# Macaron encoder trunk on one core: weights split by VectorE or by DMAs after a table, first inner tile in eight pieces, a new order

## The chip, the cores and the metric

The kernel runs on 1 core of one Trainium2 chip. The metric is the device time of one execution in microseconds; lower is better. A core has TensorE (PE in the profile; its weight loads are PEld), VectorE (DVE), ScalarE (ACT), GpSimd (POOL) and SyncE (SP). In this kernel SyncE and GpSimd issue all DMAs, GpSimd those that add into their target.

## What is computed

Two layers act on x of 512 frames by 1024 channels: a half-step SwiGLU, a mixer of parallel head groups, another half-step SwiGLU, and at the end a last RMSNorm.

```python
def reference(x, ...):
    for l in range(DEPTH):                                     # DEPTH = 2
        x = x + 0.5 * swiglu(rms_norm(x, ffn1_norm[l]), ffn1_w_in[l], ffn1_w_out[l])
        x = x + hybrid_mixer(rms_norm(x, mix_norm[l]), mix_w_in[l], ..., mix_w_out[l], pos)
        x = x + 0.5 * swiglu(rms_norm(x, ffn2_norm[l]), ffn2_w_in[l], ffn2_w_out[l])
    return rms_norm(x, final_norm)

def swiglu(h, w_in, w_out):                                    # D_FF = 2816
    gate, up = jnp.split(h @ w_in, 2, axis=-1)
    return (jax.nn.silu(gate) * up) @ w_out

def hybrid_mixer(h, w_in, ...):                                # columns of h @ w_in:
    y_conv = conv_module(u_conv, ...)        # GLU, causal depthwise conv (31 taps), LayerNorm, swish
    y_sb = stick_breaking(q_sb, k_sb, v_sb)  # 8 heads of 64
    y_r = silu(g_r) * head_norm(retention(rotary(q_r), rotary(k_r), v_r))   # 4 heads of 64
    return jnp.concatenate([y_conv, y_sb, y_r], axis=-1) @ w_out
```

All of it is float32.

## The kernel before

x stands in SBUF transposed, as eight tiles of 128 channels by 512 frames. A float32 product is made of three float32r products: each operand is split into a high part (hi, the rounded value) and the rest (lo), and hi·hi, hi·lo and lo·hi are added up in PSUM (`product`, lines 357 to 374; `block`, 523 to 538).

**Splitting a weight.** A weight unit is 128x1024 (w_in, mixer) or 128x768 and 128x640 (w_out of the half-steps). There are two ways. `weight` (line 348, `load` and `parts`): SyncE fetches it into `w_raw`, ScalarE casts it to `w_hi` (L320), VectorE subtracts to make `w_lo` (L323). `weight_by_dma` (line 339): GpSimd fetches it straight into `w_hi` (L343), ScalarE writes its negative into `w_lo` (L344), and a second DMA from GpSimd adds the weight from HBM onto it (L345). The second way needs no VectorE and reads the weight twice. Before, only the plain w_in tiles below go by DMA, 30 units in all.

**A half-step** (`ffn`) works on 22 tiles f of 128 inner channels. The first PLAIN = 4 are plain: gate and up are accumulated over the eight x tiles, in 48 products of 512 columns (`pf`), two weight units each, and the norm's factor is multiplied in afterwards (`gated`, L611 and L614). The other 18 go through `inner`, a 2x2 block scheme with seven block products instead of eight: 84 products of 256 columns (`pr`, `pu`), with sums of weight blocks, of which one is made by an adding DMA from GpSimd (L548, `w_raw`) and two by VectorE (L556). Their right-hand sides B and T are made once per half-step by `forms` (L496 to L516), and need the norm's factor `rstd`. The inner tiles are summed in four parts (PARTS) into `po` with w_out; after the last part x gets its `xh`, `xl` and square for the next norm.

**The norm** is a chain: squares summed on PE (`ss`, L462), `ms` on VectorE, a power on GpSimd (`rt`, L428), `dg` on VectorE (L440), a spreading product on PE (`bc`, L451), a copy to `rstd` on ScalarE (L470).

**The mixer** has the projections (`pj`, `pv`), the heads (`z`, ScalarE's exponentials, `y`), the conv's 31 taps on VectorE (`yc`, L1043), its LayerNorm at the end (`cmu`, `cvs`, `cbc`) and the output product in two halves (`mo`): the first half's four inputs are ready early, the second half's late.

**What sets the order.** No instruction is placed by hand. `Plan.add` records every operation with an engine and a cost, and `Plan.forward` plays them through: on every engine the lowest rank whose inputs are ready and whose buffer is free goes next. The rank is the place in the program plus `late` (DENSE_LATE for the mixer's dense products, TAPS_LATE for the conv's taps). The costs, among them the time from a DMA's issue to its landing, decide which operation the plan takes for ready; the resulting order is then fixed on every engine, and each engine works through its own list in order. Buffers are slots of rooms: 9 tiles for w_hi and w_lo, 2 for w_raw, 7 for block sums, PSUM banks 3 (mm), 4 (z) and 1 (y).

## Time and profile before

| | |
|---|---|
| time, median of 3 runs | 2015.3 us (2011.3 to 2019.25) |
| the profiled execution | 2015.95 us, its span 2014.1 us |
| mean granted TensorE clock in it | 0.974 |
| first mixer's norm sums (`ss`) | at 387.8 us |
| second half-step of layer 0, its `ss` | at 660.3 us |
| first half-step of layer 1, its `ss` | at 1014.0 us |
| second mixer's, last half-step's `ss` | at 1374.8 and 1647.0 us |
| HBM read | 268.80 MB, 134 GB/s over the span |
| instructions PE, DVE, ACT, POOL | 11522, 1961, 1534, 153 |

The profile is one execution on the chip. A row of the timeline has the start from the beginning of the span, the duration, engine, line, operation, output and inputs; in brackets the idle time of the engine before it and what ended it. The durations of matmuls overlap, since they are pipelined, so what PE can do is read from the distance of their starts and not from busy time. The view of waits sums up, for each pair of a waiting and a releasing instruction, the idle time in total, how often, and the longest. A window row has, for a stretch of time, each engine's busy time and instructions (x), the granted clock and the DMA share.

### The profile page before, as it was taken

Reading aid. Unit: us, or ns where it says so; the run is one execution under the profiler, and the core shown is the slowest. Engines: PE = TensorE matmul, PEld = TensorE weight load, DVE = VectorE, ACT = ScalarE, POOL = GpSimd, SP = SyncE. Lnnn points to the kernel's source line nnn. Section 1 sums busy time; section 2 is a strip of 40 time slices with the busy share of each in tenths; the row PEclk is TensorE's granted clock in tenths of the full one; section 3 lists DMA queues with packets and bytes.
Section 4 is the critical chain, followed back from the end, with each engine's and each line's share of the span. In section 5 each row is a group of like instructions: output and inputs, shape, how many; then the busy total and the mean of one; then the engine's idle time right before and its main releaser. Section 6 shows DMA issues by size and latency. Waiting matters only on the chain.

```text
span 2014.1 us, 29115 instructions
## 1 busy us (share of the span) xinstructions
PE 1928.1 (96%) x11522; PEld 1712.8 (85%) x11522; DVE 1373.2 (68%) x1961; ACT 973.7 (48%) x1534; POOL 148.1 (7%) x153
## 2 busy tenths in 40 slices
PE   5999999999998999999999999999999899999996
PEld 3989999788876799898779999988877788898995
DVE  5766566568997657666666666656799858565664
ACT  4535344463785434343444344445648654343442
POOL 2000000000002100000120000000000110010000
PEclk8999999999988999999999999999999999999998
DMA  9457564332417656565665565534332373575642
GB/s 268 120 152 190 152 168 140 116 105 73 116 42 174 136 140 180 152 181 144 172 147 147 157 177 154 170 112 122 85 113 64 113 157 100 152 187 152 155 131 69
DMA packets 98393, 281.19 MB, mean 140 GB/s; under 512 B 11472, under 2 KB 11984, under 8 KB 98256
## 3 DMA queue, kind: packets, MB, share of 16 engines
q1 hardware_dynamic: 70032, 210.11, 33.5%
q0 software_dynamic: 28224, 69.21, 18.4%
q8 instruction: 90, 1.47, 0.3%
q14 instruction: 47, 0.39, 0.1%
HBM read 268.80 MB, written 2.10 MB: 134 GB/s over the span
## 4 chain that ended last, share of the span: by engine, by line
PE 79%; DVE 8%; DMA 6%; issue 5%; ACT 1%; SPq 0%; POOL 0%; POOLq 0%; DVEq 0%; ACTq 0%
PE po L369 7%; PE po L368 7%; PE po L370 7%; PE pu L534 6%; PE pu L535 6%; PE pu L536 6%; PE pr L534 4%; PE pr L536 4%; PE pr L535 4%; DMA w_raw<-in_f_in 4%; PE pf L368 3%; PE pf L370 3%; PE pf L369 3%; DVE yc L1043 2%; PE z L876 2%
## 5 line engine op out<-in xcount | busy, mean ns | idle before, releaser
L320 ACT CAST w_hi<-w_raw 128x1024 fp32r<-128x1024 f32 (+2 forms) x338 | 320.3, 948 | 435.1 <-PE pu L535 124.5
L323 DVE TENSOR_TENSOR w_lo<-w_raw,w_hi 128x1024 fp32r<-128x1024 f32 (+2 forms) x338 | 369.7, 1095 | 82.5 <-ACT w_hi L320 62.9
L368 PE MATMUL po<-hh,w_hi 128*128 128x512 f32 x704 | 278.5, 396 | 10.4 <-ACT hh L320 9.6
L369 PE MATMUL po<-hl,w_hi 128*128 128x512 f32 x704 | 278.2, 395 | 1.1 <-DVE hl L323 1.1
L370 PE MATMUL po<-hh,w_lo 128*128 128x512 f32 x704 | 276.8, 393 | 1.9 <-DVE w_lo L323 1.7
L534 PE MATMUL pr<-T_hi,s_hi 128*128 128x256 f32 x576 | 162.7, 282 | 3.8 <-ACT ga L570 3.8
L368 PEld LDWEIGHTS po<-hh,w_hi 128*128 128x128 f32 x704 | 134.2, 191 | 37.0 <-ACT hh L320 10.9
L534 PE MATMUL pu<-B_hi,w_hi 128*128 128x256 f32 x576 | 162.5, 282 | 0.5 <-DVE up L583 0.5
L535 PE MATMUL pu<-B_lo,w_hi 128*128 128x256 f32 x576 | 162.5, 282 | 0.0
L536 PE MATMUL pu<-B_hi,w_lo 128*128 128x256 f32 x576 | 162.3, 282 | 0.0
L535 PE MATMUL pr<-T_lo,s_hi 128*128 128x256 f32 x576 | 162.3, 282 | 0.0
L536 PE MATMUL pr<-T_hi,s_lo 128*128 128x256 f32 x576 | 162.0, 281 | 0.0
L548 POOL DMA_DIRECT2D w_raw<-in_f_in x72 | 85.9, 1239 | 1024.4 <-DMA w_raw<-in_f_in 558.1
L370 PEld LDWEIGHTS po<-hh,w_lo 128*128 128x128 f32 x704 | 133.8, 190 | 31.2 <-DVE w_lo L323 2.7
L647 DVE SCALAR_TENSOR_TENSOR x<-po,x 128x512 f32<-128x512 f32 x128 | 88.2, 690 | 104.7 <-PE po L370 104.3
L369 PEld LDWEIGHTS po<-hl,w_hi 128*128 128x128 f32 x704 | 134.1, 190 | 27.1 <-DVE hl L323 2.6
L590 DVE TENSOR_TENSOR ga<-pu,ga 128x512 f32<-128x512 f32 x72 | 49.7, 691 | 131.4 <-PE pu L536 131.1
L368 PE MATMUL pf<-xh,w_hi 128*128 128x512 f32 x288 | 118.7, 412 | 9.9 <-ACT w_hi L320 9.9
L370 PE MATMUL pf<-xh,w_lo 128*128 128x512 f32 x288 | 115.1, 400 | 5.7 <-DMA w_lo<-in_f_in 5.6
L369 PE MATMUL pf<-xl,w_hi 128*128 128x512 f32 x288 | 114.9, 399 | 0.0
L534 PEld LDWEIGHTS pr<-T_hi,s_hi 128*128 128x128 f32 x576 | 109.3, 190 | 5.1 <-ACT ga L570 4.8
L534 PEld LDWEIGHTS pu<-B_hi,w_hi 128*128 128x128 f32 x576 | 109.4, 190 | 4.2 <-DVE up L583 1.5
(187 smaller groups left out, 4886.0 us busy)
## 6 DMA issues: line engine op xcount, KB each, us to landing
w_raw<-in_f_in SPq DMA_DIRECT2D x218, 512.0 KB, 4.3
w_raw<-in_f_in POOLq DMA_DIRECT2D x72, 512.0 KB, 6.6
w_raw<-in_f_out SPq DMA_DIRECT2D x64, 384.0 KB, 3.3
w_raw<-in_f_out SPq DMA_DIRECT2D x64, 320.0 KB, 3.0
w_raw<-in_m_in SPq DMA_DIRECT2D x36, 512.0 KB, 3.5
w_hi<-in_f_in POOLq DMA_DIRECT2D x30, 512.0 KB, 5.2
w_lo<-in_f_in POOLq DMA_DIRECT2D x30, 512.0 KB, 7.1
w_raw<-in_m_out SPq DMA_DIRECT2D x16, 512.0 KB, 3.6
```

What stands on the lines that cost most here:

```text
L320: self.a(n, lambda: nc.scalar.copy(view(hi), view(src)), [src], [hi])
L323: lambda: nc.vector.tensor_tensor(out=view(lo), in0=view(src), in1=view(hi).bitcast(F32), op=ALU.subtract),
L368: mm(acc[:], hi[:, c], h[:], start=first and a + i == 0, stop=False)
L369: mm(acc[:], hi[:, c], l[:], start=False, stop=False)
L370: mm(acc[:], lo[:, c], h[:], start=False, stop=last and a + i == len(ks) - 1)
L534: mm(out, hi[:, c], h, start=first and j + i == 0, stop=False, **opts)
L535: mm(out, hi[:, c], l, start=False, stop=False, **opts)
L536: mm(out, lo[:, c], h, start=False, stop=j + i == 2, **opts)
L548: lambda: nc.gpsimd.dma_start(rs[:].rearrange("p (a b) -> p a b", a=2), src[:, None, 2 * q : 3 * q].to_broadcast([P, 2, q]), accum_op=ALU.add,
L590: self.v(S, lambda: nc.vector.tensor_tensor(out=ga[:], in0=u[:], in1=ga[:], op=ALU.add), [u, ga], [ga])
L647: lambda x=x, po=po: nc.vector.scalar_tensor_tensor(out=x[:], in0=po[:], scalar=-0.5, in1=x[:], op0=ALU.mult, op1=ALU.add),
L876: nc.tensor.matmul(z[:, c : c + n], m[:], logs[jb][part][:, jc : jc + n], start=False, stop=i == len(todo) - 1 and part == 1, skip_group_c ...
```

## The change

- A table SPLITS gives for each of the six stages (half-step, mixer, half-step, twice) a letter per weight unit, in the order of the program: d for `weight_by_dma`, v for VectorE; units past the end of a string are v. Taken together, 93 units now go by DMA (14, 17, 15, 15, 17, 15), among them some of the mixer's and of w_out's, where there were 30, all plain w_in.
- PLAIN goes from 4 to 6 in every half-step: 16 tiles are left for `inner`.
- The very first w_in tile is loaded in eight pieces of 128x256 between the x tiles, each split by itself (`first_weights`), and ten products on a tile of zeros are put ahead of the first one (`warm`).
- The last norm leaves out the copy of `bc` to `rstd`; VectorE reads it from PSUM.
- The plan's costs: DMAs from GpSimd share the planned bus with SyncE's, other DMA times, 0.119 us for a product of 256 columns, 0.09 us more for `xh`; DENSE_LATE 100 to 240, TAPS_LATE 400 to 380, one more slot in the room f. Every engine's order comes out anew.

```diff
--- before.py
+++ after.py
@@ -24,12 +24,22 @@
 N_UNITS = 24
 EPS = 1e-6
 NEG = -(2.0**100)
-N_F, N_R, N_RAW, N_W, N_WS = 19, 45, 2, 9, 7
-PLAIN = 4
+N_F, N_R, N_RAW, N_W, N_WS = 20, 45, 2, 9, 7
+PLAIN = 6
 AHEAD = 1
-DENSE_LATE, TAPS_LATE = 100, 400
+SPLITS = {
+    0: "dvvvdvdvdvdvddvvvdvvddvvvdvvdvvvvvvvdvvd",
+    1: "vvvdvddvdddvvvvddddvddvdvdddd",
+    2: "dvddvvdvddvvvvvvvdvdvdvvvdvvvdvvvvvdddd",
+    3: "dvddvvdvddvvvvvvvdvdvdvvvdvvvdvvvvvdddd",
+    4: "vvvdvddvdddvvvvddddvddvdvdddd",
+    5: "dvddvvdvddvvvvvvvdvdvdvvvdvvvdvvvvvdddd",
+}
+DENSE_LATE, TAPS_LATE = 240, 380
 PARTS = ((0, 6), (6, 12), (12, 17), (17, 22))
 HS = S // 2
 TT = S // P
@@ -221,7 +231,7 @@
                     cost += LOAD if tables else 0.0
                     tables = o.table
                 o.start, idle[e] = now, now + cost
-                if e == "sync":
+                if isinstance(o.lag, tuple):
                     bus = max(bus, now + cost) + o.lag[0]
                     o.end = bus + o.lag[1]
                 else:
@@ -231,7 +241,7 @@
                 done += 1
                 for a in o.after:
                     left[a] -= 1
-                    t = o.end + (SIGNAL if ops[a].engine != e or e == "sync" else 0.0)
+                    t = o.end + (SIGNAL if ops[a].engine != e or isinstance(o.lag, tuple) else 0.0)
                     ready[a] = max(ready[a], t)
                     if not left[a]:
                         heapq.heappush(queues[ops[a].engine], (rank[a], a))
@@ -297,19 +307,20 @@
         self.tc, self.nc, self.io, self.out = tc, tc.nc, io, out
         self.plan = Plan()
         self.late = 0
+        self.modes = SPLITS[0]
     def v(self, n, fn, r, w, inputs=1, late=0):
         return self.plan.add("vector", vec(n, inputs), fn, r, w, late=late)
-    def a(self, n, fn, r, w, table=None, after=()):
-        return self.plan.add("scalar", sca(n), fn, r, w, table=table, after=after)
+    def a(self, n, fn, r, w, table=None, after=(), more=0.0):
+        return self.plan.add("scalar", sca(n) + more, fn, r, w, table=table, after=after)
     def pe(self, cost, fn, r, w, late=0):
         return self.plan.add("tensor", cost, fn, r, w, lag=0.17, late=late)
     def dma(self, size, fn, r, w):
-        return self.plan.add("sync", 0.33, fn, r, w, lag=(size / 350e3, 1.7))
+        return self.plan.add("sync", 0.33, fn, r, w, lag=(size / 330e3, 1.9))
     def tile(self, room, name, shape=(P, S), dtype=F32):
         return Buf(room, list(shape), dtype, name)
@@ -334,19 +345,23 @@
     def add_dma(self, n, fn, out):
-        self.plan.add("gpsimd", 0.9, fn, [out], [out], lag=n * P * 4 / 250e3 + 4.0)
+        self.plan.add("gpsimd", 1.1, fn, [out], [out], lag=(n * P * 4 / 200e3, 3.8))
     def weight_by_dma(self, src, n=KT * P):
         nc = self.nc
         hi, lo = (self.tile(self.w, name, (P, KT * P), F32R) for name in ("w_hi", "w_lo"))
-        self.plan.add("gpsimd", 0.6, lambda: nc.gpsimd.dma_start(hi[:, :n], src), [], [hi], lag=n * P * 4 / 250e3 + 2.6)
+        self.plan.add("gpsimd", 0.6, lambda: nc.gpsimd.dma_start(hi[:, :n], src), [], [hi], lag=(n * P * 4 / 300e3, 2.9))
         self.a(n, lambda: nc.scalar.activation(lo[:, :n], hi[:, :n].bitcast(F32), ACT.Copy, scale=-1.0), [hi], [lo])
         self.add_dma(n, lambda: nc.gpsimd.dma_start(lo[:, :n], src, accum_op=ALU.add), lo)
         return hi, lo, 0
     def weight(self, src, n=KT * P):
+        by_dma = self.modes[:1] == "d"
+        self.modes = self.modes[1:]
+        if by_dma:
+            return self.weight_by_dma(src, n)
         return (*self.parts(self.load(src, n), n, "w"), 0)
     def parts(self, raw, n, name, room=None):
@@ -396,7 +411,7 @@
         if g is not None:
             xh, xl = (self.tile(self.r2, n, dtype=F32R) for n in ("xh", "xl"))
             self.xs.append((xh, xl))
-            self.a(S, lambda: nc.scalar.activation(xh[:], x[:], ACT.Copy, scale=g[:, d : d + 1]), [x, g.buf], [xh])
+            self.a(S, lambda: nc.scalar.activation(xh[:], x[:], ACT.Copy, scale=g[:, d : d + 1]), [x, g.buf], [xh], more=0.09)
             self.v(
                 S,
                 lambda: nc.vector.scalar_tensor_tensor(
@@ -451,7 +466,7 @@
         self.pe(0.86, lambda: self.nc.tensor.matmul(bc[:], self.ones[:], dg[:], start=True, stop=True), [self.ones, dg], [bc])
         return bc
-    def norm(self, room):
+    def norm(self, room, last=False):
         nc, acc = self.nc, self.acc
         ps = self.bank(room, "ss")
@@ -466,6 +481,9 @@
         self.pe(0.13 * TT * len(acc), sums, [*acc, self.ones], [ps])
         self.r = self.inv_sqrt(ps, TT, 1.0 / D)
         bc = self.spread(self.r, room, "bc")
+        if last:
+            self.rstd = bc
+            return
         rstd = self.rstd = self.tile(self.f2, "rstd")
         self.a(S, lambda: nc.scalar.copy(rstd[:], bc[:]), [bc], [rstd])
@@ -473,11 +491,33 @@
-    def plain(self, src, weight=None):
+    def plain(self, src):
         q = KT * P // 2
-        (h0, l0, _), (h1, l1, _) = ((weight or self.weight)(src[:, c : c + 2 * q]) for c in (0, 2 * q))
+        (h0, l0, _), (h1, l1, _) = (self.weight(src[:, c : c + 2 * q]) for c in (0, 2 * q))
         return [[(h0, l0, 0), (h1, l1, q)], [(h1, l1, 0), (h0, l0, q)]]
+    def first_weights(self, src, j):
+        q, n, out = KT * P // 2, 2 * P, []
+        for block in ((0, 2), (3, 1))[j // 2]:
+            raw, hi, lo = self.tile(self.f2, "wf", (P, n)), *(self.tile(self.r2, f"wf_{p}", (P, n), F32R) for p in ("hi", "lo"))
+            at = block * q + j % 2 * n
+            self.dma(n * P * 4, lambda raw=raw, at=at: self.nc.sync.dma_start(raw[:], src[:, at : at + n]), [], [raw])
+            self.split(raw, n, hi, lo)
+            out.append((hi, lo))
+        return out
+    def warm(self, n):
+        t, ps = self.tile(self.r2, "zeros", dtype=F32R), self.bank(self.y, "warm")
+        self.v(S, lambda: self.nc.vector.memset(t[:].bitcast(F32), 0.0), [], [t])
+        def fn():
+            for i in range(n):
+                self.nc.tensor.matmul(ps[:], t[:, :P], t[:], start=i == 0, stop=i == n - 1)
+        self.pe(0.6 * n, fn, [t], [ps])
     def forms(self, g):
@@ -535,7 +575,7 @@
                     mm(out, hi[:, c], l, start=False, stop=False, **opts)
                     mm(out, lo[:, c], h, start=False, stop=j + i == 2, **opts)
-            self.pe(2 * 3 * HS * COLUMN, fn, [hi, lo, bh, bl], [acc], self.late)
+            self.pe(2 * 3 * 0.119, fn, [hi, lo, bh, bl], [acc], self.late)
     def inner(self, src, b, hs):
@@ -618,10 +658,10 @@
             )
             self.gate(ga, up, pair(f))
-        banks = [self.products(first or self.plain(w_in[0], self.weight_by_dma), (self.mm, self.z))]
+        banks = [self.products(first or self.plain(w_in[0]), (self.mm, self.z))]
         self.norm(self.y)
         for f in range(1, PLAIN):
-            units = self.plain(w_in[f], self.weight_by_dma)
+            units = self.plain(w_in[f])
             accs = [self.bank(room, "pf") for room in (self.mm, self.z)]
             for acc, unit in zip(accs, units):
                 for h in range(2):
@@ -1187,10 +1227,13 @@
             x = self.x[d]
             self.dma(262144, lambda: nc.sync.dma_start(x[:], io["x"][:, d, :]), [], [x])
-        load_x(0)
-        first = self.plain(io["f1_in"][0][0])
-        for d in range(1, KT):
-            load_x(d)
+        self.warm(10)
+        first = [[], []]
+        for j in range(4):
+            load_x(2 * j)
+            for unit, (hi, lo) in zip(first, self.first_weights(io["f1_in"][0][0], j)):
+                unit.append((hi, lo, 0))
+            load_x(2 * j + 1)
         for d in range(KT):
             self.x_ready(d, g[0])
         self.ident = const("ident", [P, P])
@@ -1219,14 +1262,18 @@
         def half_step(name, l, gain, after, first=None):
             self.ws = self.plan.room("ws", N_WS, self.plan.stage, loose=3)
             self.ffn(io[f"{name}_in"][l], io[f"{name}_out"][l], gain, after, first)
+            next_stage()
+        def next_stage():
             plan.next_stage()
+            self.modes = SPLITS.get(plan.stage, "")
         for l in range(DEPTH):
             half_step("f1", l, g[3 * l], lambda d: self.x_ready(d, g[3 * l + 1]), None if l else first)
             self.mixer(l, lambda d: self.x_ready(d, g[3 * l + 2]))
-            plan.next_stage()
+            next_stage()
             half_step("f2", l, g[3 * l + 2], lambda d: self.x_ready(d, g[3 * l + 3] if l < DEPTH - 1 else None))
-        self.norm(self.y)
+        self.norm(self.y, True)
         gl, rstd = g[3 * DEPTH], self.rstd
         for d in range(KT):
             o, x = self.tile(self.f2, f"o{d}"), self.x[d]
```

**GpSimd at the start of the program.** `w_hi` is a fetch, `w_lo` an adding DMA of a weight, `w_raw` the adding DMA of a block sum, `rt` the norm's power. Before:

```order
L343 DMA w_hi<-in_f_in 128x1024 x5
L548 DMA w_raw<-in_f_in 128x2x512 x4
L428 ISA
L428 TENSOR_TENSOR rt<-ms,mhalf 128x4
L345 DMA w_lo<-in_f_in 128x1024 x4
L343 DMA w_hi<-in_f_in 128x1024
```

and now:

```order
L354 DMA w_hi<-in_f_in 128x1024 x4
L354 DMA w_hi<-in_f_out 128x768
L356 DMA w_lo<-in_f_in 128x1024
L588 DMA w_raw<-in_f_in 128x2x512
L443 ISA
L443 TENSOR_TENSOR rt<-ms,mhalf 128x4
L588 DMA w_raw<-in_f_in 128x2x512 x3
```

One adding DMA of a weight has come ahead of the power, and only one block sum is left ahead of it instead of four. On PE, the spreading product `bc` that this power leads to stood directly behind the first tile's 48 products; now 12 products of the second tile, with a weight that VectorE splits, stand between.

**PE at the end of the first half-step of layer 0.** `pu` is the last block product of tile 21, `hh` and `hl` with the numbers 3562 and 3564 (now 3490 and 3498) are that tile's result. Before:

```order
L534 MATMUL pu_3347<-B21_hi_459,w_hi_3279 128x256
L535 MATMUL pu_3347<-B21_lo_489,w_hi_3279 128x256
L536 MATMUL pu_3347<-B21_hi_459,w_lo_3304 128x256
L368 MATMUL po_3434<-hh_3562,w_hi_3327 128x512
L369 MATMUL po_3434<-hl_3564,w_hi_3327 128x512
L370 MATMUL po_3434<-hh_3562,w_lo_3336 128x512
```

and now, from the seventeenth row behind the last `pu`:

```order
L384 MATMUL po_3482<-hl_3447,w_hi_3326 128x512
L385 MATMUL po_3482<-hh_3439,w_lo_3410 128x512
L383 MATMUL po_3399<-hh_3490,w_hi_3233 128x512
L384 MATMUL po_3399<-hl_3498,w_hi_3233 128x512
L385 MATMUL po_3399<-hh_3490,w_lo_3268 128x512
```

Before, the tile's result was needed by the row right behind its last block product; now 18 rows of `po` with older tiles stand between the last `pu` and it.

**PE at the end of the first mixer.** `y` is the last head's product, `cvs` and `cbc` belong to the conv's LayerNorm, `rbc` to the norm of a retention head, `mo` is the output product. Before:

```order
L826 MATMUL y<-wl,vs 128x256
L826 MATMUL y<-wl,vs 128x512
L1069 MATMUL cvs<-avg,csq 128x1 x8
L451 MATMUL cbc<-dg,ones 128x512
L982 MATMUL rbc<-c_ident,ex 128x128 x4
L368 MATMUL mo<-yh,w_hi 128x512
```

and now, around `cbc`:

```order
L916 MATMUL z<-lh,mones 128x128
L916 MATMUL z<-ll,mones 128x128
L466 MATMUL cbc<-dg,ones 128x512
L916 MATMUL z<-lh,r_tri 128x256
L916 MATMUL z<-ll,r_tri 128x256
L916 MATMUL z<-lh,mones 128x128
L916 MATMUL z<-ll,mones 128x128
```

`cvs`, `cbc` and `rbc` have moved ahead of the last head's `y`. 18 rows (12 `mo`, 6 `z`) stand between `cvs` and `cbc`, and 18 more between `cbc` and `rbc`.

## The prediction

> **What bounds the kernel now.** The page's busy line and its chain of waits come first.
>
> ```profile
> PE 1928.1 (96%) x11522; PEld 1712.8 (85%) x11522; DVE 1373.2 (68%) x1961; ACT 973.7 (48%) x1534; POOL 148.1 (7%) x153
> PE 79%; DVE 8%; DMA 6%; issue 5%; ACT 1%; SPq 0%; POOL 0%; POOLq 0%; DVEq 0%; ACTq 0%
> ```
>
> PE is the bound nearly everywhere: 79% of the chain. A change can therefore win in two ways: fewer products, or shorter stretches in which PE waits. VectorE at 68% is relief only where PE waits for it. Those places are in the view of waits, PE's own:
>
> ```profile
> PE pf L368 <- ACT w_hi L320: 9.9, 2, 9.3
> PE po L368 <- ACT hh L320: 9.6, 4, 3.4
> PE bc L451 <- DVE dg L440: 9.3, 2, 6.9
> PE pr L536 <- DVE w_lo L323: 7.2, 2, 3.6
> PE cbc L451 <- DVE dg L440: 6.8, 2, 3.4
> PE z L798 <- ACT wt L842: 5.7, 4, 1.8
> PE pf L370 <- DMA w_lo<-in_f_in: 5.6, 1, 5.6
> PE mo L368 <- ACT yh L320: 4.4, 2, 2.2
> PE ss L462 <- DVE sq L411: 2.8, 2, 2.6
> ```
>
> These are some 61 us, few and long. Each long one is paid a second time, which windows of equal length show.
>
> ```profile
> 363.30:368.30 5.00, 5.00 (x13) 3.94 (x12) 3.16 (x5) 4.26 (x7) 0.57 (x1) 0.50 0.39 105
> 370.00:375.00 5.00, 5.00 (x24) 4.14 (x23) 3.90 (x7) 1.98 (x3) 0.00 (x0) 1.00 0.24 64
> 695.00:700.50 5.50, 1.89 (x9) 1.46 (x9) 5.50 (x9) 2.39 (x4) 0.00 (x0) 0.90 0.00 0
> 700.50:705.50 5.00, 5.00 (x25) 5.00 (x25) 2.15 (x4) 1.42 (x3) 0.00 (x0) 0.50 0.66 194
> 705.50:710.50 5.00, 5.00 (x41) 5.00 (x41) 2.95 (x4) 2.68 (x4) 0.00 (x0) 0.92 0.39 124
> ```
>
> Right after the 3.4 us wait for `hh`, PE gets through 13 matmuls in 5 us, and a little later 24 of the same kind in as long; after the 3.6 us wait for `w_lo`, 25 against 41. So the granted clock was 0.50 for some 5 us behind each. What that costs is the missing matmuls times the distance of two starts, which the timeline of PE gives:
>
> ```profile
> 695.06 0.39 PE L369 MATMUL pf<-xl,w_hi 128*128 128x512 f32 x1
> 695.29 0.39 PE L370 MATMUL pf<-xh,w_lo 128*128 128x512 f32 x1
> ...
> 356.04 0.28 PE L535 MATMUL pu<-B_lo,w_hi 128*128 128x256 f32 x1
> 356.16 0.28 PE L536 MATMUL pu<-B_hi,w_lo 128*128 128x256 f32 x1
> ```
>
> About 0.227 us for 512 columns and 0.119 us for 256 (the rows are rounded to 0.01; these are means over longer stretches). So the first wait costs 3.4 + 11 x 0.227 = 5.9 us, the second 3.6 + 16 x 0.119 = 5.5 us.
>
> The Trainium skill (TensorE: Matmul & The Clock Gate, Part 1: The HAM clock gate) has the clock halved after an idle window of about 3.4 us and back after as long a busy one. By that a wait would cost 1.7 us more, an estimate from the page; the windows show 1.9 and 2.5, and I take theirs. With the page's figure the sum below would gain some 3 us less.
>
> **The change, part by part.** The sum is made against the profiled execution, 2015.95 us (span 2014.1); the median of the runs is 2015.3, which is the same within 0.1%.
>
> *The head of the program: 12 us less.*
>
> ```profile
> 9.30:26.90 17.60, 16.95 (x64) 12.02 (x64) 11.12 (x16) 10.63 (x19) 3.60 (x3) 1.00 1.05 373
> 42.50:47.40 4.90, 4.89 (x12) 3.79 (x13) 4.90 (x10) 0.62 (x1) 0.00 (x0) 0.50 1.06 211
> ...
> 25.48 1.17 POOL L548 DMA_DIRECT2D w_raw<-in_f_in  x1 [0.81 <-DMA w_raw<-in_f_in]
> 27.83 1.50 POOL L428 TENSOR_TENSOR rt<-ms,mhalf 128x4 f32<-128x4 f32 x1
> ...
> 33.00 0.87 DVE L440 TENSOR_SCALAR dg<-c_ident,rt 128x128 f32<-128x128 f32 x4
> 36.77 0.48 DVE L496 SCALAR_TENSOR_TENSOR B<-x,c_gains,rstd 128x256 f32<-128x256 f32 x1 [2.30 <-ACT rstd L470]
> 59.73 0.69 DVE L611 TENSOR_TENSOR ga<-pf,rstd 128x512 f32<-128x512 f32 x1
> ...
> 34.02 2.04 PE L451 MATMUL bc<-dg,ones 128*128 128x512 f32 x2 [6.95 <-DVE dg L440]
> 42.51 0.80 PE L370 MATMUL pf<-xh,w_lo 128*128 128x512 f32 x1 [5.59 <-DMA w_lo<-in_f_in]
> ```
>
> Before, 64 matmuls of the first tile and its norm are through by 26.9; then PE waits 6.95 us for `dg` and 5.59 us for a `w_lo` that comes by DMA, and from 42.5 it works at half clock. I give the eight pieces and the zeros nothing by themselves: ScalarE's order now has the negation of a DMA weight ahead of the first cast, and the x tiles' casts and squares are strung up behind, so the first tile ends where it did, a us or so earlier. (Bounds: 0 to 4 us, the first wait of 9.3 us being mostly the arrival of data.) What moves is the norm: `rt` stood behind four adding DMAs, now behind one, whose data is third in SyncE's queue as that of the row at 25.48 was; and `dg` no longer stands on VectorE behind two sums that wait for data. So: adding DMA at 25.5, `rt` from 26.7 to 28.2, `dg` to 29.1, `bc` to 30.1 instead of 36.1. By then 12 products of the second tile are done, since their weight is split by VectorE, and the `w_lo` that PE needs next was issued behind the fetches of the start, not behind four block sums. At 30.1 PE has 60 products behind it; before, it had 60 at 42.5 + 10 x 0.41 = 46.6 (12 matmuls in the 4.9 us from 42.5). That is 16.5 us. What is late next: the fourth tile needs a PSUM bank that `ga` frees, and `ga` stands on VectorE behind the forms, 59.73 - 36.77 = 23 us after `rstd`, now with three weight splits more (3.7 us): 30.8 + 26.6 = 57.4. PE arrives there after 36 + 48 + 24 products, at 54.6, waits 2.8 us and may lose 2 us of clock. 16.5 - 4.8 = 12, rounded. (5 to 17.)
>
> *Ends of the first half-steps: 11.8 us less.* 18 `po` (4.1 us) stand where PE waited 3.4 us for `hh`. 5.9 us twice.
>
> *First inner tile behind a mixer: 11 us less.* PE waited 3.6 us for `w_lo` while VectorE was busy all the time (5.50 of 5.50 above) with the forms. Two plain tiles more are 22 us of PE work ahead of that place. 5.5 us twice.
>
> *End of the second half-step of layer 0: 5 us less.* Nine products of the next tile now stand ahead of `ss`, which waited 2.6 us; with the clock behind it, 2.4.
>
> *The mixers: 23.6 us less.*
>
> ```profile
> 388.00:611.00 223.00, 217.98 (x1102) 184.58 (x1102) 184.40 (x287) 142.15 (x247) 3.66 (x3) 0.98 0.30 85
> 611.00:628.00 17.00, 10.80 (x45) 7.40 (x44) 12.62 (x24) 9.28 (x13) 8.51 (x6) 0.79 0.93 270
> ```
>
> In the second row only 45 matmuls fit into 17 us: PE waits 3.4 us for `cbc` and 2.2 us for `mo`, with nothing else to do since the last head is through. The new order has these two links inside the last head's work, with 18 rows of other work behind each; 3.4 + 2.2 + 2.4 of clock = 8.0. This needs the conv's taps earlier on VectorE: 17 weights by DMA take 17 x 1.1 = 19 us off it, of 184 busy in 223. Of the waits for `wt` (2.85 us a mixer) I let half go, with one half-clock stretch, 2.4. Together 11.8, twice. (4 to 20 each.)
>
> *The last norm: 0.6 us less.*
>
> ```profile
> 2004.12 0.59 ACT L470 COPY rstd<-bc 128x512 f32<-128x512 f32 x1 [6.29 <-PE bc L451]
> ```
>
> The copy is alone on the path.
>
> *Two more plain tiles: 7.2 us more.* A plain tile is 48 x 0.227 = 10.9 us, an inner one 84 x 0.119 = 10.0; eight change over. The zeros run before any data is there.
>
> *63 more weights by DMA: 12 us more.*
>
> ```profile
> L323 DVE TENSOR_TENSOR w_lo<-w_raw,w_hi 128x1024 fp32r<-128x1024 f32 (+2 forms) x338 | 369.7, 1095 | 82.5 <-ACT w_hi L320 62.9
> ...
> L548 POOL DMA_DIRECT2D w_raw<-in_f_in x72 | 85.9, 1239 | 1024.4 <-DMA w_raw<-in_f_in 558.1 <-DVE w_lo L323 104.6 <-ACT bb L570 76.1
> L345 POOL DMA_DIRECT2D w_lo<-in_f_in x30 | 26.2, 986 | 86.3 <-ACT w_lo L344 80.0 <-DVE sq L411 4.7 <-ACT rstd L470 1.6
> L343 POOL DMA_DIRECT2D w_hi<-in_f_in x30 | 17.5, 588 | 155.6 <-PE pf L370 76.8 <-PE po L370 36.2 <-ACT sp L842 25.9
> ...
> w_raw<-in_f_in SPq DMA_DIRECT2D x218, 512.0 KB, 4.3
> w_hi<-in_f_in POOLq DMA_DIRECT2D x30, 512.0 KB, 5.2
> w_lo<-in_f_in POOLq DMA_DIRECT2D x30, 512.0 KB, 7.1
> ```
>
> A weight by DMA takes 5.2 + 1.05 (ScalarE) + 7.1 us from its first issue, by VectorE 4.3 + 1.05 + 1.1: some 7 us longer, hidden as long as it is asked for in time. GpSimd's own work stays small: 93 x (0.59 + 0.99) + 64 x 1.24 = 226 us. But each adding DMA waits there for ScalarE, and behind it stand the fetches, the block sums and `rt`. Of 30 such weights one made PE wait, 5.6 us, or 0.19 us a weight; 63 more at that rate are 12. (0, if the order covers all of them, to 40, if one in ten comes with its whole 7 us.)
>
> Sum: 12 + 11.8 + 11 + 5 + 23.6 + 0.6 - 7.2 - 12 = 44.8 us less, **1971 us**.
>
> **The rivals.**
> - *VectorE frees the mixers further: 1955.* If the first row's 223 us for 1102 matmuls are VectorE's (184 busy, the rest dependencies on it), 19 us less work shorten them too; 8 us more a mixer. Against it: PE had hardly a wait of over 2 us there.
> - *The covers hold only in part: 2003.* The new order, like the old one, is made from estimated costs, and the old one left waits where those were off. If half of the 64 us of gains come back as other waits, 1971 + 32.
> - *Weights by DMA come late: slower, 2028.* The mechanism is GpSimd's in-order queue: an adding DMA that waits for ScalarE holds up the block sum behind it, which `s_hi`, `r2` and so a whole inner tile need. It decides from 0.19 + 44.8/63 = 0.9 us for each added weight, where nothing is left of the gain; at 1.1 us the time is 1971 + 69 - 12. For it: GpSimd goes from 132 such DMAs to 250. Against it: PE's list has one wait for a DMA.
> The Trainium skill (SBUF — State Buffer, two separate sides) names a way to this: VectorE's two-port operations lock GpSimd out while it writes descriptors. The rows bear it out little, 0.59, 0.99 and 1.24 us an issue beside a VectorE that is 68% busy, so it adds nothing to this rival's chance.
> - *The change does little on balance: 2012.* The half-steps' ends stay, since the chain behind `hh` grows by a late `w_lo`.
>
> **How the numbers follow.** Forecast 0.50 (1955 to 1988 on its own), VectorE 0.17, half 0.20, late 0.07, little 0.06. The range of 8 in 10 goes from 1947 (VectorE's rival, with the head at its best and a few us of the 12 for late weights not needed) to 2007 (halved gains and a few more late weights). Half a per cent, about what a measurement can tell here, is 10 us: faster, below 2005, has the forecast, VectorE and most of the half, 0.82; same 0.10; slower 0.08.
>
> **What would show it.** `bc` at about 29 instead of 34 us and no wait for `w_lo` by DMA before it; PE's waits for `hh` below 1 us at the first half-steps' ends; no 3.6 us wait of `pr` for `w_lo`; a mixer from `ss` to `ss` of about 261 us instead of 272.5, `cbc` and `mo` without waits over 1 us; all plain and inner products together 7 us longer. The forecast is wrong if PE's list has many waits for `w_lo` or `w_raw` by DMA, or if GpSimd's waits for ScalarE grow and `s` is late behind them.

## The result and the profile after

| | before | after |
|---|---|---|
| time, median | 2013.93 us (4 runs, 2011.30 to 2019.25) | 1950.23 us (4 runs, 1943.95 to 1953.31) |
| ratio | | 0.9676, 95% interval 0.9644 to 0.9709 |
| profiled execution, span | 2015.95, 2014.1 us | 1949.24, 1947.5 us |
| mean granted clock | 0.974 | 0.990 |
| first `ss` of each later stage | 387.8, 660.3, 1014.0, 1374.8, 1647.0 | 373.2, 623.9, 976.4, 1327.8, 1581.6 |

The kernel is 64 us faster, 3.2%. The forecast was 45 us; the time lies in its range (1947 to 2007), near the lower end, and below the 1955 to 1988 that the forecast had on its own. First the busy line and the chain of waits of the changed kernel:

```profile
PE 1909.4 (98%) x11244; PEld 1688.6 (87%) x11244; DVE 1285.4 (66%) x1873; ACT 953.9 (49%) x1499; POOL 226.7 (12%) x271
PE 87%; DVE 5%; DMA 3%; issue 2%; ACT 2%; SPq 0%; POOLq 0%; POOL 0%; DVEq 0%; ACTq 0%
```

PE's share of the chain went from 79% to 87%. PE has 278 matmuls fewer and yet more columns to work through: eight inner tiles of 84 short products became plain ones of 48 long ones. VectorE has 88 us less work. The view of PE's waits, whose columns are the total, how often, and the longest:

```profile
PE z L838 <- ACT wt L882: 4.6, 4, 2.6
PE pf L383 <- ACT wf_hi L331: 4.2, 3, 2.0
PE ss L477 <- DVE sq L426: 3.0, 3, 1.5
PE z L838 <- DVE rt L944: 2.4, 2, 1.2
PE bc L466 <- DVE dg L455: 2.4, 1, 2.4
...
PE pr L574 <- ACT ga L610: 1.5, 1, 1.5
...
PE pf L383 <- DVE ga L651: 1.4, 1, 1.4
PE po L385 <- DVE w_lo L334: 0.9, 1, 0.9
```

All the long ones of before are gone: no wait for `hh`, none for `w_lo` by DMA, none of `pr` for `w_lo`, none of `cbc` or `mo`. The one `bc` left is that of the last norm. None lasts longer than 2.6 us. The windows, with the granted clock as the first number behind POOL's:

```profile
26.90:42.50 15.60, 15.60 (x75) 12.79 (x75) 10.44 (x21) 6.49 (x10) 6.31 (x5) 1.00 1.09 255
...
345.00:350.00 5.00, 4.78 (x20) 3.47 (x19) 2.31 (x4) 3.15 (x4) 0.00 (x0) 1.00 0.24 66
...
562.00:624.00 62.00, 61.22 (x306) 50.82 (x304) 50.26 (x83) 45.39 (x76) 11.30 (x12) 1.00 0.63 152
```

The kernel before in the first of these stretches:

```profile
26.90:42.50 15.60, 3.06 (x5) 1.17 (x4) 8.46 (x20) 8.98 (x13) 5.88 (x6) 0.72 1.16 218
```

From 26.9 to 42.5, where it started 5 matmuls, there are now 75. Behind the first half-step's last inner tile there are 20 in 5 us at full clock, where there were 13 at half. The end of the first mixer, 62 us with 306 matmuls, has PE busy for 61.22 of them; before, 45 matmuls took 17 us there.

**Where the time went, as a sum.** From the trace, for every matmul: the distance to the next start, less the usual distance of its shape (the 30th percentile in the changed kernel), summed up. That is the time in which PE isn't at its own pace. The time before the first product and the matmuls on zeros count as lost; what comes behind the start of the last matmul (11.2 us before, 10.3 after) counts in neither. What is left is the work itself, 1842.6 us with PLAIN 4 and 1850.1 with PLAIN 6.

| lost, us | first half-step with the start | mixer 0 | second half-step | first, layer 1 | mixer 1 | last, and the end |
|---|---|---|---|---|---|---|
| before | 40.2 | 33.7 | 19.9 | 13.2 | 33.5 | 20.2 |
| after | 22.2 | 21.0 | 7.0 | 3.3 | 23.4 | 10.3 |

The half-steps lose 50.7 us less, the mixers 22.8, and the work is 7.5 longer: 66.0 of the 66.6 us between the two spans. The rest is the end behind the last matmul.

### The profile page after: what moved, and what is told of

Same layout as the page of the kernel before. It is cut to its first block, busy times and chain, and to the rows that moved or that the text cites. A ratio compares the mean times of both kernels' runs of the same rounds, so it can differ in the third digit from the quotient of the medians.

```text
span 1947.5 us, 28438 instructions
## 1 busy us (share of the span) xinstructions
PE 1909.4 (98%) x11244; PEld 1688.6 (87%) x11244; DVE 1285.4 (66%) x1873; ACT 953.9 (49%) x1499; POOL 226.7 (12%) x271
## 4 chain that ended last, share of the span: by engine, by line
PE 87%; DVE 5%; DMA 3%; issue 2%; ACT 2%; SPq 0%; POOLq 0%; POOL 0%; DVEq 0%; ACTq 0%
PE po L384 7%; PE po L383 7%; PE po L385 7%; PE pu L574 6%; PE pu L575 6%; PE pu L576 6%; PE pf L383 5%; PE pf L384 5%; PE pf L385 5%; PE pr L574 5%; PE pr L575 5%; PE pr L576 5%; DVE yc L1083 2%; PE pj L383 2%; PE pj L384 2%
## 5 line engine op out<-in xcount | busy, mean ns | idle before, releaser
L331 ACT CAST w_hi<-w_raw 128x1024 fp32r<-128x1024 f32 (+2 forms) x273 | 260.7, 957 | 237.2 <-DMA w_raw<-in_f_in 73.5
L334 DVE TENSOR_TENSOR w_lo<-w_raw,w_hi 128x1024 fp32r<-128x1024 f32 (+2 forms) x273 | 302.0, 1108 | 60.4 <-ACT w_hi L331 27.1
L383 PE MATMUL pf<-xh,w_hi 128*128 128x512 f32 x400 | 159.4, 399 | 1.4 <-DVE ga L651 1.4
L385 PE MATMUL pf<-xh,w_lo 128*128 128x512 f32 x400 | 156.4, 391 | 0.0
L384 PE MATMUL pf<-xl,w_hi 128*128 128x512 f32 x400 | 156.3, 391 | 0.0
L574 PE MATMUL pr<-T_hi,s_hi 128*128 128x256 f32 x512 | 144.3, 282 | 1.5 <-ACT ga L610 1.5
L575 PE MATMUL pu<-B_lo,w_hi 128*128 128x256 f32 x512 | 144.4, 282 | 0.0
L574 PE MATMUL pu<-B_hi,w_hi 128*128 128x256 f32 x512 | 144.4, 282 | 0.0
L355 ACT ACTIVATE w_lo<-w_hi 128x1024 fp32r<-128x1024 f32 (+2 forms) x93 | 88.4, 951 | 69.3 <-DMA w_hi<-in_f_out 20.1
L635 ACT ACTIVATE ga<-ga 128x512 f32<-128x512 f32 x88 | 55.2, 632 | 129.9 <-DVE ga L630 104.1
```

What stands on the lines that cost most here:

```text
L331: self.a(n, lambda: nc.scalar.copy(view(hi), view(src)), [src], [hi])
L334: lambda: nc.vector.tensor_tensor(out=view(lo), in0=view(src), in1=view(hi).bitcast(F32), op=ALU.subtract),
L355: self.a(n, lambda: nc.scalar.activation(lo[:, :n], hi[:, :n].bitcast(F32), ACT.Copy, scale=-1.0), [hi], [lo])
L383: mm(acc[:], hi[:, c], h[:], start=first and a + i == 0, stop=False)
L384: mm(acc[:], hi[:, c], l[:], start=False, stop=False)
L385: mm(acc[:], lo[:, c], h[:], start=False, stop=last and a + i == len(ks) - 1)
```

## The experiments

Twelve kernels were run, in three sets, each beside runs of the kernel before (medians 2011.34, 2013.69 and 2013.73 us). All of them have their order planned anew from the edit, so that each run tells what the edit and the new order do together. The lost time is that of the table above, summed over the four half-steps and over the two mixers.

| kernel | time, us | ratio to before, 95% interval | lost in half-steps | in mixers |
|---|---|---|---|---|
| before | 2013.93 | | 93.5 | 67.2 |
| after | 1950.23 | 0.9676 (0.9644 to 0.9709) | 42.8 | 44.4 |
| e9: old due times | 1948.42 | 0.9675 (0.9658 to 0.9692) | 45.5 | 39.1 |
| e2: first tile as before | 1950.23 | 0.9699 (0.9683 to 0.9715) | 43.9 | 43.0 |
| e3: PLAIN 4 | 1963.75 | 0.9771 (0.9752 to 0.9790) | 67.9 | 41.2 |
| e1: mixer weights by VectorE | 1966.98 | 0.9781 (0.9766 to 0.9795) | 43.8 | 61.6 |
| e6: before, new costs alone | 1986.09 | 0.9861 (0.9846 to 0.9876) | 70.8 | 60.2 |
| e12: before's 30 in half-steps | 1988.80 | 0.9884 (0.9866 to 0.9902) | 80.9 | 46.8 |
| e11: 123 weights by DMA | 1992.83 | 0.9889 (0.9867 to 0.9912) | 88.7 | 43.7 |
| e4: old costs and due times | 1997.97 | 0.9935 (0.9919 to 0.9951) | 69.3 | 64.8 |
| e10: even places | 1998.51 | 0.9930 (0.9915 to 0.9945) | 93.5 | 43.4 |
| e5: half-step weights by VectorE | 2005.73 | 0.9961 (0.9946 to 0.9977) | 89.7 | 54.6 |
| e13: old costs of DMAs | 2008.00 | 0.9976 (0.9958 to 0.9993) | 70.9 | 67.6 |
| e8: all 238 by DMA | 2062.62 | 1.0231 (1.0207 to 1.0255) | 139.5 | 63.7 |

**e1: the mixers' weights by VectorE.**

```diff
-    1: "vvvdvddvdddvvvvddddvddvdvdddd",
-    4: "vvvdvddvdddvvvvddddvddvdvdddd",
```

> The changed kernel with all of the mixers' weights split by VectorE; the half-steps' tables, the head, PLAIN = 6 and the plan's costs stay. Theory (the mixers gained because 17 weights a mixer left VectorE, so the conv's taps are done before the last head): VectorE gets some 19 us a mixer back, the mean and norm of the conv come behind the last head again, PE waits for cbc and mo by 2 to 3 us each, and each mixer is 6 to 11 us longer; 12 to 22 us more in all, 1962 to 1972. Rival (the order's other numbers, DENSE_LATE and the costs, made the mixers shorter): within 5 us of 1950, no wait of PE for cbc or mo.

Measured 1966.98 us, and the loss sits in the mixers alone: 61.6 us lost against 44.4. Its waits and the window at the end of the first mixer:

```profile
PE mo L381 <- ACT yh L329: 4.3, 2, 3.0
...
PE cbc L464 <- DVE dg L453: 2.1, 2, 1.9
PE cmu L1092 <- DVE yc L1081: 2.0, 1, 2.0
```

```profile
578.00:640.00 62.00, 56.80 (x245) 45.45 (x245) 46.94 (x74) 32.67 (x50) 11.00 (x9) 0.92 0.57 131
```

245 matmuls in 62 us where the changed kernel has 306. The waits that the prediction named (`cbc`, `mo`) come back, with one of `cmu` for the conv's own sum `yc`: the taps are late again. So with these costs the mixers' gain needs their weights off VectorE.

**e2: the first tile as before, no matmuls on zeros.**

```diff
-        self.warm(10)
-        first = [[], []]
-        for j in range(4):
...
+        load_x(0)
+        first = self.plain(io["f1_in"][0][0])
```

> The changed kernel with the first inner tile loaded as before (two units of 128x1024, split by VectorE, ahead of x1 to x7) and no products on zeros. Theory (the head gained by the norm's place and by a second tile whose weights are not late by DMA): 0 to 5 us more, 1950 to 1955, bc at 32 to 34 us and no wait of PE for a w_lo by DMA. Rival (the eight pieces and the zeros are what gained): 10 us or more, with PE some 10 us behind at 60 us of the span.

Measured 1950.23 us, the median of the changed kernel. The eight pieces and the zeros are worth nothing that these runs can tell: the first half-step with the start loses 24.7 us instead of 22.2, and the later stages a little less. One sign that I had named failed: `bc` comes at 27.5 us, five us sooner than in the changed kernel, but then PE waits 4.0 us for a `w_lo` by DMA, at 36.0. The two heads lose nearly the same in different places.

**e3: PLAIN 4.** The letters of the two inner tiles that are no longer plain are taken out of the table.

```diff
-PLAIN = 6
+PLAIN = 4
```

> The changed kernel with PLAIN = 4, the letters of the fifth and sixth plain tile taken out of the tables. Theory (six plain tiles are paid with 7 us of products and save the wait of the first inner tile): the products get 7 us shorter, and behind each mixer PE waits 3 us or more for w_lo or for the forms, with half clock after it, so 0 to 8 us more, 1950 to 1958. Rival (the plain tiles are a loss by themselves): 7 us less, 1943, without such waits.

13 us slower, more than I expected. The wait that the two plain tiles were to cover is back, as PE's list shows:

```profile
PE pr L576 <- DVE w_lo L334: 15.1, 5, 5.5
```

It is 3.5 us long behind each mixer, as before the change (3.6), and 5.5 us in the very first half-step, where the kernel before had none. So beside this table PLAIN 6 buys 25.1 us less lost in the half-steps with 7.5 us more work. That it is needed with any table isn't shown: e6 below has PLAIN 4 and no such wait.

**e4: before's costs and due times, the rest as changed.** The planner's costs of DMAs, of ScalarE's copies and of the half-width products, and the two due times, are set back.

```diff
-DENSE_LATE, TAPS_LATE = 240, 380
+DENSE_LATE, TAPS_LATE = 100, 400
-                if isinstance(o.lag, tuple):
+                if e == "sync":
-        self.plan.add("gpsimd", 1.1, fn, [out], [out], lag=(n * P * 4 / 200e3, 3.8))
+        self.plan.add("gpsimd", 0.9, fn, [out], [out], lag=n * P * 4 / 250e3 + 4.0)
...
```

> The changed kernel planned with the costs, DENSE_LATE and TAPS_LATE of before; tables, head and PLAIN as changed. Theory (each part removes its own wait, and the costs only help the order to hold): 0 to 15 us more, 1950 to 1965. Rival (the gain is the better plan): 25 us or more of the 64 come back, 1975 or later, as waits of PE for hh, w_lo and the conv's norm.

1997.97 us: with the same table, the same PLAIN and the same start, three quarters of the gain are gone. The mixers lose nearly what they lost before the change (64.8 us), the half-steps stand halfway back (69.3).

**e9: the old due times alone.**

```diff
-DENSE_LATE, TAPS_LATE = 240, 380
+DENSE_LATE, TAPS_LATE = 100, 400
```

> The changed kernel with the two due times of before (DENSE_LATE 100, TAPS_LATE 400) and all else as changed, the costs too: the order differs in the mixers alone (872 lines on PE). If the due times carry the mixers' gain, both mixers lose again what they lost with the old costs (about 10 to 13 us each): 1970 to 1976. If the costs do, it is 1950 to 1956.

1948.42 us, its interval within that of the changed kernel: the due times carry nothing that these runs can tell. What e4 lost hangs on the costs.

**e13: the old costs of DMAs alone.**

```diff
-                if isinstance(o.lag, tuple):
+                if e == "sync":
-        self.plan.add("gpsimd", 1.1, fn, [out], [out], lag=(n * P * 4 / 200e3, 3.8))
+        self.plan.add("gpsimd", 0.9, fn, [out], [out], lag=n * P * 4 / 250e3 + 4.0)
...
```

> The changed kernel whose planner has before's costs of DMAs only (GpSimd's take no share of the DMA bandwidth and land sooner after their issue: 0.9 and 0.6 us of issue, 4.0 and 2.6 us after their data at 250 GB/s; plain loads at 350 GB/s); its costs of ScalarE's copies and of the half-width products, and the due times, are the changed ones. With all old costs the time was 1998. If the DMAs' costs carry that loss (the planner puts weights too late, so PE waits for w_lo by DMA and for what stands behind it): 1985 to 2000. If the two compute costs carry it: 1950 to 1962.

2008.00 us (10 runs, 1999.79 to 2015.82; the profiled one took 2000.05). The mixers lose 67.6 us, as before the change, but not at the same places: PE has no wait for `cbc` and 1.7 us for `mo`. In its list of PE's waits the weights by DMA are late:

```profile
PE pf L385 <- DMA w_lo<-in_f_in: 14.3, 3, 7.2
PE pu L574 <- DVE up L623: 9.4, 6, 2.3
```

One of the three is in the head, 7.2 us. The other two, 3.6 us each, stand at the ends of the mixers, where the order has put the first plain tile of the next half-step ahead of `ss`. A planner that believes a weight by DMA to be there sooner than it is puts its product too early. But e13 isn't faster than e4, where the compute costs are old as well: the effects of the parts don't add up.

**e6: the kernel before with the new costs and due times.**

```diff
-DENSE_LATE, TAPS_LATE = 100, 400
+DENSE_LATE, TAPS_LATE = 240, 380
-        self.plan.add("gpsimd", 0.9, fn, [out], [out], lag=n * P * 4 / 250e3 + 4.0)
+        self.plan.add("gpsimd", 1.1, fn, [out], [out], lag=(n * P * 4 / 200e3, 3.8))
...
```

> The kernel before with nothing changed but the planner's costs and the two due times (DENSE_LATE 240, TAPS_LATE 380): no table, PLAIN 4, first tile and last norm as before. If the plan by itself carries what the run with the old costs lost (some 48 us), the time is 1960 to 1970. If plan and table work only together (a better order needs the weights early, and in the mixers they come from VectorE here), the mixers lose what they lost with all their weights on VectorE (some 22 us over both against the changed kernel), PLAIN 4 some 13, and the time is 1980 to 1992. If the costs only help where the table is, it stays within 2005 to 2015.

1986.09 us, in the range of the second case, though not by its parts: against the changed kernel the mixers lose 15.8 us more, not 22, and the half-steps 28.0, not 13. PE has no wait for `cbc` here, 1.6 us for `mo` and, with PLAIN 4, no wait of `pr` for `w_lo`. So the order that the new costs make covers these links without a table. What the mixers lose has moved: 30.7 us of their 60.2 stand at `z`, where it was 25.7 before and 18.2 after the change, counted as in the table. In all, the costs and due times alone bring 28 us, the rest alone (e4, with e9 to say that the due times don't matter) 13 to 16, both together 64.

**e5: the half-steps' weights by VectorE.**

```diff
-    0: "dvvvdvdvdvdvddvvvdvvddvvvdvvdvvvvvvvdvvd",
-    2: "dvddvvdvddvvvvvvvdvdvdvvvdvvvdvvvvvdddd",
...
+    0: "",
```

> The changed kernel, but every weight of the four half-steps is split by VectorE (59 weights go back from DMA to VectorE); the mixers' 34 stay on DMA. The table of the half-steps is the disputed part. If the planned order carries most of the gain by itself (as the run with the old costs suggested), VectorE has room in the half-steps (it is busy 66% of the span) and the time is 1952 to 1965. If the freed VectorE is what ends the half-steps' small waits, 59 x 1.1 us = 65 us of VectorE's time come back, waits of the products of the inner tiles for w_lo by VectorE appear as they did with PLAIN 4, and the time is 1970 to 1990.

2005.73 us (10 runs), even more than the second case. PE waits for a PSUM bank that `ga` on VectorE has to free, in the fourth plain tile, and for `ga` in the inner ones:

```profile
PE pf L380 <- DVE ga L648: 15.4, 3, 5.9
PE pr L571 <- ACT ga L607: 9.8, 7, 2.8
```

But in the second half-step `ga` isn't late: it comes 35.2 us behind `ss`, in the changed kernel 34.8. The new order has 48 plain products ahead of this `ss` instead of 12, so PE is through with the 168 that the free banks take before `ga` comes. It is the same in both half-steps of layer 1 (45 and 48 instead of 9 and 12). So these waits are the order's; what VectorE's lack of time costs by itself isn't shown. And as this run has less by DMA in the half-steps than even the kernel before, it says that they need some with this planner, not how many.

**e12: only before's 30 weights by DMA in the half-steps.**

```diff
-    2: "dvddvvdvddvvvvvvvdvdvdvvvdvvvdvvvvvdddd",
+    2: "dddddddd",
...
```

> The changed kernel with, in the half-steps, only the weights by DMA that the kernel before had (those of the first four inner tiles, 6 and 8 a half-step, 30 in all; the table has 59); PLAIN 6, the mixers' letters, the costs and the first tile stay as changed. If the added 29 weights of the half-steps are what ends the small waits there, it loses about half of what the run with none by DMA lost (56 us): 1970 to 1985. If only the weights of the first inner tiles matter (the run with none by DMA lost most there, where PE waited 15 us for ga by VectorE), it is 1952 to 1965.

1988.80 us, just beyond the first case. The places have changed along with the number here, and PE waits 10.0 us for `w_lo` by DMA in the first four plain tiles, whose weights all come that way.

**e10: as many by DMA, at even places.**

```diff
-    2: "dvddvvdvddvvvvvvvdvdvdvvvdvvvdvvvvvdddd",
+    2: "vvdvvdvdvvdvdvvdvvdvdvvdvdvvdvvdvdvvdvd",
...
```

> The changed kernel with as many weights by DMA in each stage as the table has (14 and 15 in the half-steps, 17 in each mixer), but spread evenly over the same letters instead of where the table puts them; the order is planned anew for it. If it is VectorE's freed time that counts (as the runs with all mixer weights and all half-step weights on VectorE suggest), even places do nearly as well: 1952 to 1968. If the places are what counts (a weight by DMA helps only where VectorE is late), it gives back a large part: 1972 to 2000.

1998.51 us. The mixers don't care (43.4 us lost against 44.4), the half-steps lose all they had gained: 93.5, as before the change. Windows of equal length at the same place, first e10's and then the changed kernel's, some 20 to 35 us behind `ss` in the second half-step:

```profile
665.00:680.00 15.00, 10.13 (x42) 8.02 (x41) 14.49 (x25) 6.58 (x11) 0.55 (x1) 0.84 0.47 127
```

```profile
644.00:659.00 15.00, 15.00 (x68) 12.43 (x67) 12.73 (x24) 7.16 (x10) 2.83 (x4) 1.00 0.55 142
```

With two weight splits among the forms instead of one VectorE is busy for 14.49 of 15 us, and PE waits 4.9 us for the bank that `ga` frees. Here are `ga` and PE's product in e10, and then `ga` in the changed kernel:

```profile
677.36 0.68 DVE L651 TENSOR_TENSOR ga<-pf,rstd 128x512 f32<-128x512 f32 x1
678.10 0.80 PE L383 MATMUL pf<-xh,w_hi 128*128 128x512 f32 x1 [4.87 <-DVE ga L651]
...
658.69 0.69 DVE L651 TENSOR_TENSOR ga<-pf,rstd 128x512 f32<-128x512 f32 x1
```

The splits are not the cause: `ga` comes 32.8 us behind `ss` in e10 and 34.8 in the changed kernel. As in e5 it is PE that is there sooner, since 54 plain products stand ahead of this `ss` instead of 12 (42 and 54 in layer 1, instead of 9 and 12). In the changed kernel only 154 have started when `ga` comes, and the banks hold. The other loss is at the half-steps' ends. The timeline of e10, in the order PE, VectorE, ScalarE, PE (in brackets the idle time of the engine before the row), and as its last line the window behind it:

```profile
354.84 0.28 PE L576 MATMUL pu<-B_hi,w_lo 128*128 128x256 f32 x1
...
355.15 0.69 DVE L630 TENSOR_TENSOR ga<-pu,ga 128x512 f32<-128x512 f32 x1 [8.46 <-PE pu L576]
...
356.29 0.62 ACT L635 ACTIVATE ga<-ga 128x512 f32<-128x512 f32 x1
356.94 1.28 ACT L1068 ACT_TABLE_LOAD   x1
358.23 0.62 ACT L331 CAST hh<-up 128x512 fp32r<-128x512 f32 x1
...
358.90 0.79 PE L383 MATMUL po<-hh,w_hi 128*128 128x512 f32 x1 [3.79 <-ACT hh L331]
359.63 0.79 PE L384 MATMUL po<-hl,w_hi 128*128 128x512 f32 x1
...
359.00:364.00 5.00, 5.00 (x11) 3.65 (x12) 2.51 (x4) 2.36 (x4) 1.09 (x2) 0.50 0.52 126
```

From the last inner product to `hh` it takes some 4 us, and nothing stands in between on PE; behind it PE is at half clock, 11 matmuls in the 5 us from 359.0. The changed kernel has the same gap (last inner product from 344.18, `hh` from 347.85 to 348.47), and 18 `po` of other tiles in it, so that PE runs on. Which letters make the planner keep them for this place wasn't tried.

**e11: 30 more by DMA.** Every fourth v of the table becomes a d.

```diff
-    1: "vvvdvddvdddvvvvddddvddvdvdddd",
+    1: "vvvddddvdddvvdvddddvddvdddddd",
...
```

> The changed kernel with every fourth v of the table turned into d: 123 weights by DMA instead of 93 (the run with all 238 took 2063 us and PE waited there 31 us for w_lo by DMA). If lateness starts only where the GpSimd queue is near its limit, this is 1948 to 1960, PE without waits for DMA. If each further weight by DMA costs something (the 113 us between 93 and 238 are 0.78 us a weight), it is 1965 to 1980, with waits of PE for w_lo by DMA.

1992.83 us, beyond the second case. PE waits 10.1 us in four places for `w_lo` of the first tiles by DMA and 11.1 for `hh` at the ends. One of the first, in the timeline (ScalarE, GpSimd, PE):

```profile
661.24 1.06 ACT L355 ACTIVATE w_lo<-w_hi 128x1024 fp32r<-128x1024 f32 x1 [1.54 <-PE pf L385]
...
662.60 0.86 POOL L356 DMA_DIRECT2D w_lo<-in_f_in  x1 [0.78 <-ACT w_lo L355]
...
669.81 0.79 PE L385 MATMUL pf<-xh,w_lo 128*128 128x512 f32 x1 [2.72 <-DMA w_lo<-in_f_in]
670.40 0.63 PE L383 MATMUL pf<-xh,w_hi 128*128 128x512 f32 x1
```

The copy that opens a `w_lo` had to wait until PE's last product with an older weight left its tile free; from there it is 8.6 us to the product. By VectorE the same step is a subtraction of 1.2 us. So in this place a weight by DMA holds one of the nine tiles that much longer before it is of use. That tiles alone set the limit isn't shown. The window from the copy to the product has the DMA engines at a share of 0.96; it was 0.55 in the changed kernel's window above:

```profile
661.00:670.00 9.00, 6.28 (x28) 4.89 (x28) 8.97 (x17) 5.82 (x9) 2.81 (x4) 0.97 0.96 210
```

**e8: all 238 weights by DMA.**

```diff
-    0: "dvvvdvdvdvdvddvvvdvvddvvvdvvdvvvvvvvdvvd",
+    0: "d" * 60,
...
```

> The changed kernel with every weight that the table holds brought by a plain and an adding DMA: 237 weights (93 in the changed kernel). VectorE loses 144 more splits (about 160 us of its busy time), ScalarE gains 144 copies, GpSimd 288 DMA issues. My theory (the weights by DMA cost nothing as long as they are ahead; the planner counts their queue): nothing late, 1945 to 1956. Rival (the GpSimd queue works in order and waits there for ScalarE's copies and for free buffers, so more than some share of the weights comes late): waits of PE for w_lo by DMA appear, each some us, and the time is 1965 to 2010.

2062.62 us, slower than the kernel before, though VectorE has only 1154.9 us to do. PE's list:

```profile
PE po L385 <- DMA w_lo<-in_f_out: 30.8, 22, 8.2
PE pf L385 <- DMA w_lo<-in_f_in: 8.9, 4, 3.0
```

So weights that come late by DMA, as the slower rival of the prediction had them, are real at 145 weights more, 0.78 us each (112 us through 145). What PE waits for is `w_lo` itself, not the block sums that the rival named, and the 39.7 us in the list are a third of the loss; the rest wasn't traced. At the 93 of the table none of it shows.

## Why the prediction was right, point by point

The sign and the mechanism held: PE bounds, and its few long waits with their half clock were to go. The sum was too small by 22 us. Against the table of lost time:

- **The head (12):** right in size, in part by luck. Together with the first half-step's end it was 17.9, measured 18.0 (40.2 to 22.2), of which 12.1 up to 64 us. The timeline of the changed kernel:

```profile
27.98 1.20 POOL L588 DMA_DIRECT2D w_raw<-in_f_in  x1 [19.02 <-DMA w_raw<-in_f_in]
28.81 1.85 POOL L443 TENSOR_TENSOR rt<-ms,mhalf 128x4 f32<-128x4 f32 x1
...
30.70 1.00 DVE L455 TENSOR_SCALAR dg<-c_ident,rt 128x128 f32<-128x128 f32 x4 [0.94 <-DMA w_raw<-in_f_in]
...
32.51 1.02 PE L466 MATMUL bc<-dg,ones 128*128 128x512 f32 x2
...
58.69 0.69 DVE L651 TENSOR_TENSOR ga<-pf,rstd 128x512 f32<-128x512 f32 x1
...
59.43 0.50 PE L383 MATMUL pf<-xh,w_hi 128*128 128x512 f32 x1 [1.41 <-DVE ga L651]
```

  The first tile didn't end a us earlier, as I had it: `ss` began at 26.6 instead of 23.7, and `ms` was there at 28.6. `rt` stood behind one adding DMA, whose data came at 28.0 and not at 25.5; so `bc` was at 32.5, not 30.1, but behind products and without a wait. The wait for the PSUM bank that I named as next was there, 1.41 us instead of 2.8, since `ga` came at 58.7 (57.4 predicted) and PE later than I had it; the 2 us of clock weren't lost. So 2.4 us lost and 3.4 us not lost nearly cancelled. That the pieces and zeros by themselves bring nothing, e2 shows.
- **Ends of the first half-steps (11.8):** held. `po` for `hh` is gone. e10, e11 and e12, where the cover is missing, have the wait back.
- **First inner tile behind a mixer (11) against PLAIN 6 (+7.2):** held for this table. The work is 7.5 us longer, and e3 brings the wait back. But e6, with PLAIN 4 and other weights by DMA, doesn't have it either.
- **The mixers (23.6):** 22.8, but from other parts. At `cbc`, `mo` and `rbc` the loss fell from 27.4 to 4.7, 22.7 where I had 16; at `z` by 7.5, as I had it (7.6); and at the other products it grew by 7.3, where I had nothing. Part of the reason held: with the 17 weights back on VectorE the gain is lost (e1). But the two links alone don't need that, since e6 covers them with all weights on VectorE, and its mixers lose elsewhere. That the gain also needs the planner to know what a DMA costs (e13) stood nowhere in the prediction.
- **63 more weights by DMA (+12): the mis-sized term.** It took 0.19 us a weight from the one late weight of before. PE's list after has no wait for a DMA at all, so it measured 0, the lower bound given. The sign that I named for it misled: GpSimd's waits for ScalarE did grow sixfold, from 80.0 us,

```profile
POOL w_lo L356 <- ACT w_lo L355: 481.7, 77, 21.5
```

  and PE waited for nothing behind them; VectorE's waits for the block sums' data (`s`) even fell, from 74.1 to 44.1 us. Nor is the price one per weight: it is 0 at 93, and e11 and e8 show PE waiting 12.2 us for `w_lo` by DMA at 123 and 39.7 at 238.
- **The rest, 11 us more than predicted,** is in the half-steps: 4.0 in the first of layer 1 (9.9 instead of 5.9; the clock behind its `ss`, 2.4, I had put to the stage before), 2.4 in the second one of layer 0 (12.9 instead of 10.5) and 4.4 in the last (9.9 instead of 5.5). I had priced four of the long waits there and left out the short ones, such as those of `pr` for `ga` (3.8 us in five before, 1.5 in one after) and the smaller half of `po`'s for `hh`.
- **Two side sums** in the prediction are off, and neither enters the forecast: with 1.7 us of clock for each wait the terms give some 5 us less, not 3, and one in ten of 63 weights at 7 us is 44 us, not 40.

The rival that VectorE would free the mixers further was near in time, 1955, and wrong in place: the mixers gave no more than the forecast. The sign that I had named would speak for it: from `ss` to `ss` the mixers took 250.7 and 253.8 us, where the forecast had 261 and this rival 253. But these windows have less work in them as well. 12 plain products of the next half-step instead of 45 stand ahead of their last `ss`, and 6 and 3 more products ahead of their first one, together 8.9 and 8.2 us at 0.227 us each. The rival that half the covers fail, 2003, is what seven of the experiments look like (1986 to 2008); the changed kernel escaped it through its particular order.

What stays open: why just this table, with these costs, gives a half-step order without gaps. Each change to the table or PLAIN in the half-steps (e3, e5, e8, e10, e11, e12) cost 13 to 112 us. The waits tell what each of them broke, the first tiles or the ends or both, but not which letter does it, nor why the order then has 48 or 54 plain products ahead of `ss`. No run beat the changed kernel by more than the intervals allow.

## What to carry to other kernels

When a list scheduler sets the order, an ingredient has no worth of its own: costs alone brought 28 us, all the rest without them 13 to 16, both 64, and the same number of weights moved to even places lost three quarters of it. Measure such a change as a whole, and look in each stage for the place where PE stands still: here the bank freed by `ga` behind the forms, and the last `hh`. Ask there whether the wait's end came late or PE came early: in e5 and e10 it was PE. And off-loading has a limit: a transfer that takes 8.6 us where the engine took 1.2 needs its buffer that much earlier, and at 123 weights by DMA some were late.
